# First stage of a two-layer decoder trunk: input, sixteen modulation rows and the first weights in one DRAM array

## The chip, the cores and the metric

The kernel runs on one core of a Trainium2 chip. The metric is the device time of one execution in microseconds (us). Five engines work side by side, each on its own queue: TensorE (PE in the profile, with its weight loads as PEld), VectorE (DVE), ScalarE (ACT), GpSimd (POOL) and SyncE (SP), which here issues nearly all DMAs. Engines wait for each other and for DMAs through semaphores.

## The reference

A trunk of two layers for one sequence of 256 tokens and model width 1024. Each layer is a half-step SwiGLU block, a token mixer (stick-breaking attention in layer 0, an RG-LRU recurrence in layer 1), and another half-step SwiGLU block; each of them starts from a normalised input that is scaled and shifted by a conditioning vector.

```python
mod = (c_act @ mod_w[layer] + mod_b[layer]).reshape(B, N_SUB, 3, D_MODEL)
shift, scale, gate = mod_j[:, 0], mod_j[:, 1], mod_j[:, 2]
h = rmsnorm(x, g) * (1 + scale[:, None, :]) + shift[:, None, :]
g, u = jnp.split(h @ w_gu, 2, axis=-1)
x = x + MACARON_W * (1 + gate) * ((jax.nn.silu(g) * u) @ w_down)
```

Only the very first block matters here: it needs the input `x` (1 MB), the conditioning vector `c`, the shift and scale of sub-layer 0 (two products of `c` with a 1024 x 1024 matrix of `mod_w`) and the weights `w_gu`.

## The kernel before, in words

The input is held transposed: 8 tiles `x[d]` of 128 rows of the model dimension by 256 tokens, in one buffer in on-chip memory (SBUF). Weights are float32. Each weight piece is loaded into `raw` (three buffers of 8 KB a partition), split by ACT into a rounded part `wh` (L555) and by DVE into the rest `wl` (L558), and multiplied in three passes by `Acc.group` (L584). The modulation is not computed by TensorE: each 128 x 1024 tile of the transposed `mod_w` is loaded, and one DVE instruction multiplies it by the activated vector and sums along the row (`mod_tile`, L616). One such tile gives one column, the 128 shifts or scales of one `x[d]`.

The order of work is not written by hand. The program lists its operations with costs and dependences; `Program.schedule` simulates the engines and sorts the operations by their simulated start. The costs of DMAs come from the size alone (`c_dma`), and the address is no part of it. A chain of `after` dependences (`chained`, and `last` in `early`) fixes the order of the first stage's DMAs on SP's queue. Every transfer is recorded by the helper `dma` and so has line L521.

The first stage reads, on SP's queue, in this order: the input in two halves (the second half carries 72 columns of parameters behind each row), the first scale tile (`w` = 1) and the first shift tile (`w` = 0), and then for each of the eight steps k of the model dimension the 128 x 2048 weights `gu0[k]`, in 512-column pieces for k = 0, 1, 3 and 7 and in 1024-column pieces for the others. Each half of a step's weights is followed by a modulation tile of the next step (for k up to 4), scale after the first half and shift after the second; for k of 5 and 6 both follow the first half. While this runs, ACT forms the two modulation columns `mf`, then the modulated input `hx` and `hpre` of step k (L528); DVE forms the rest of it (L907); TensorE multiplies it into eight banks, one for each of the first eight tiles of the hidden dimension. The first half of the weights of step 0 is multiplied unsplit (L883). Eight DMAs of SP can be on the way: a further one waits for the one issued eight before it.

Where these sources lie: `xT` is one array of 128 rows of 2120 columns, and each half is a column range of it. `modw` is an array of 2 x 72 tiles, each 128 x 1024 and contiguous; the 16 tiles of the first stage are two runs of 8. `gu0` holds for each k a contiguous 128 x 2048 block, and a piece is a column range of it: rows of 2 KB or 4 KB, 8 KB apart.

After the first stage the kernel streams the remaining weights in 1 MB loads and multiplies them; it takes some 95% of the time and isn't touched by the change.

Of the kernel before, what the change touches and what calls it, by code (L numbers as in the profile page):

```python
# [14 lines left out]
P = 128  # L15
T = 256
TX = T + 2
D = 1024
KD = D // P
# [10 lines left out]
CH = 2048  # L30
HALF = 1024
SQ = 8
NFIRST = 2
LAT0, RATE0, RATE = 1250.0, 390.0, 360.0
LAT1 = 2050.0
LASTY = 900.0
SMALL = (0,1,3,7)
# [15 lines left out]
NP0 = OFF_MB + 3 * KD  # L53
# [312 lines left out]
        return sorted(order, key=lambda o: o.start)  # L366


def c_act(n, psum=False, ptr=0):
    return (51.0 if psum else 93.0) + 0.8333 * n + 93.0 * ptr  # L370

# [11 lines left out]


@with_exitstack
def trunk(ctx, tc, xT, cb, par, modw, gu0, gu, wdn, qk, wv, wo, win, wri, wout, out):
    nc = tc.nc
    act, dve, pe, pool, sp = nc.scalar, nc.vector, nc.tensor, nc.gpsimd, nc.sync
    ctx.enter_context(tc.manual_schedule())
# [84 lines left out]
    xall = fixed("x", KD * T + NPAR)  # L474
    x = [Buf(ap=xall[:, d * T : (d + 1) * T]) for d in range(KD)]
    cact = Buf(ap=fixed("cact", D))
    pars = Buf(ap=xall[:, KD * T :])
# [42 lines left out]
    def dma(dst, src, n, w, after=(), lat=None, rate=RATE):  # L520
        return pr.op("DMA", c_dma(n, rate), lambda: sp.dma_start(dst(), src), w=w, after=after, lat=lat)  # L521
# [12 lines left out]
    def load(src, n, name, chain=None, size=HALF, plain=0, homes=(), behind=(), kind=Buf):  # L534


        homes = list(homes)
        raw = Buf(rawr, name=f"raw_{name}")
        part = None
        if chain is None:  # L540
            dma(lambda: raw()[:, :n], src, n, [raw])
        res = []
        for a in range(0, n, size):
            m = min(n - a, size)
            if chain is not None:
                part = a
                chain(lambda a=a, m=m: raw()[:, a : a + m], src[:, a : a + m], m, [(raw, a)])
            if len(res) < plain:
                res.append((raw, part))
                continue  # L550
            h, lo = (Set(homes.pop(0), 9) if homes else kind(ring_, name=f"{w}_{name}")
                     for ring_, w in ((whr, "wh"), (wlr, "wl")))

            def fh(h=h, a=a, m=m):
                act.activation(h()[:, :m], raw()[:, a : a + m], AF.Copy)  # L555

            def fl(h=h, lo=lo, a=a, m=m):
                dve.tensor_tensor(lo()[:, :m], raw()[:, a : a + m], f32(h()[:, :m]), ALU.subtract)  # L558

            pr.op("ACT", c_act(m), fh, [(raw, part)], [h], behind if res else ())  # L560
            V(fl, m, [(raw, part), h], [lo])
            res.append((h, lo))
        return res
# [45 lines left out]
    def mod_tile(l, s, w, t, after=(), lat=None, rate=RATE, home=None, behind=()):  # L609

        m = mraw[l, s, w]
        raw = home or Buf(modr)
        load_ = dma(raw, modw[l, (s * 3 + w) * KD + t], D, [raw], after, lat, rate)

        def fn():
            dve.scalar_tensor_tensor(raw(), raw(), 1.0, cact(), ALU.mult, ALU.mult, accum_out=m()[:, t : t + 1])  # L616
        V(fn, D, [raw, cact] + list(behind), [raw, (m, t)])
        return load_
# [226 lines left out]
    def ffn(l, s, nxt, hook):  # L845
# [12 lines left out]
        if j == 0:  # L858
# [3 lines left out]
            q = rstd((0, 0))  # L862
# [49 lines left out]
            for k in range(KD):  # L912
                if k == 0:
                    h0 = norm_chunk((0, 0), k, q, PLAIN > 0)
                    warm(LATE, [pr.last_pe])
                    for ks in xq_parts[:2]:
                        normed(ks)
                    copied = ()
                else:
                    copied = [first_chunk(k)]  # L920
                size = HALF // 2 if k in SMALL else HALF
                done = [0]

                def chain(dst, src, n, w):
                    chained(dst, src, n, w, RATE0, LAT0 if k < 3 else LAT1)
                    done[0] += n

                    if done[0] % HALF == 0:
                        for w in ((2 - done[0] // HALF,) if k < 5 else (1, 0) if done[0] == HALF else ()):
                            early(k + 1, w)  # L930

                plain = PLAIN if k == 0 else 0
                ws = load(gu0[k], CH, f"gu0_{k}", chain, size, plain, (), copied if k == 1 else ())
                if k == 1:
                    normed(xq_parts[2], [ws[0][1].hist[None][0]])
                other = copies(*hcur[0, 0][k]) if k in COPIED else None
                for f in range(SQ):
                    h = other if other and f == 2 else hcur[0, 0][k]
                    for g in range(2):
                        i, c0 = divmod((f * 2 + g) * P, size)  # L940
                        if i < plain:
                            plain_group(accs[f], g, *ws[i], (f * 2 + g) * P)
                            continue
                        group(accs[f], (g, 0), lambda b, g=g: b[:, g * T : (g + 1) * T], ws[i],
                              lambda u, c0=c0: u[:, c0 : c0 + P], h, lambda v: v[:, :T], T, k == KD - 1)
                        if k in KICK0 and f == g == 0:
                            kick_op(accs[f], 0, (0, 0))
# [439 lines left out]
    def chained(dst, src, n, w, rate=RATE, lat=LAT0):  # L1387
        last[:] = [dma(dst, src, n, w, last, lat, rate)]
# [10 lines left out]
    def first_loads(F):  # L1399
        c, b = Buf(modr), [Buf(banks), Buf(banks)]  # L1400
        act_dma(lambda: c()[:1, :], cb, [], [c], 300.0)

        def cond(h, after=()):
            cs = slice(h * 512, (h + 1) * 512)
            A(lambda: cact()[:, cs], b[h], AF.Silu, 512, [b[h]], [(cact, h)], table="silu", psum=True, after=after)

        warm(EARLY)
        for h in range(2):
            cs = slice(h * 512, (h + 1) * 512)
            pr.op("PE", 1870.0, lambda h=h, cs=cs: pe.matmul(b[h]()[:, :], ones[:1, :], c()[:1, cs], start=True, stop=True),  # L1410
                  [c], [b[h]])
        cond(0)
        warm(MID, [pr.last_pe])


        pairs = []
        for h, (scalar_, vector_, extra) in enumerate(((0, 2, 0), (2, 0, NP0))):
            d = 4 * h
            a0, n = d * T, 4 * T + extra
            chained(lambda a0=a0, n=n: xall[:, a0 : a0 + n], xT[:, a0 : a0 + n], n, x[d : d + 4] + [(pars, 0)] * h, RATE0)  # L1420
            sq = Buf(F, 8)
            v0 = vector_ * T
            V(lambda sq=sq, a0=a0, v0=v0: dve.tensor_tensor(
                sq()[:, v0 : v0 + 2 * T], xall[:, a0 + v0 : a0 + v0 + 2 * T], xall[:, a0 + v0 : a0 + v0 + 2 * T], ALU.mult),
              2 * T, x[d + vector_ : d + vector_ + 2], [(sq, "V")])
            for i in (scalar_, scalar_ + 1):
                o = A(lambda sq=sq, i=i: sq()[:, i * T : (i + 1) * T], x[d + i], AF.Square, T, [x[d + i]], [(sq, i)])
            if h == 1:
                cond(1, [o])
            p = Buf(F, 4)  # L1430
            V(lambda sq=sq, p=p: dve.tensor_tensor(p(), sq()[:, : 2 * T], sq()[:, 2 * T :], ALU.add), 2 * T,
              [(sq, "V"), (sq, scalar_), (sq, scalar_ + 1)], [p])
            if h == 0:
                pairs += [(p, slice(0, T)), (p, slice(T, 2 * T))]
            else:
                one = Buf(F, 2)
                fold = V(lambda p=p: dve.tensor_tensor(one(), p()[:, :T], p()[:, T:], ALU.add), T, [p], [one])
                pairs.append((one, slice(0, T)))
        ssq[0, 0] = tuple(pairs)
        pr.op("DVE", 80.0, lambda: dve.scalar_tensor_tensor(gbias(), col(OFF_MB + KD, KD), 1.0, col(OFF_NG, KD), ALU.add,  # L1440
                                                            ALU.mult), [(pars, 0)], [gbias], [fold])
# [4 lines left out]
    rate = {0: (1.4, SQ, 30), 1: (1.25, 0, 8), 2: (1.3, 0, 32), 3: (1.3, 0, 32)}  # L1446
# [38 lines left out]
def _layout(i):  # L1485
# [9 lines left out]
        [cols(i[n]) for n in ("norm_g", "mod_b", "final_norm_g", "lru_conv_w", "lru_conv_b", "lru_b_r", "lru_b_i",  # L1495
                              "lru_lambda")], axis=1)
    a["par"] = c(par[:, NP0:])
    a["xT"] = c(np.concatenate([i["x"].reshape(T, KD, P).transpose(2, 1, 0).reshape(P, KD * T), par[:, :NP0]], axis=1))
    a["modw"] = c(i["mod_w"].transpose(0, 2, 1)).reshape(2, 9 * KD, P, D)
    gu = i["ffn_w_gu"].reshape(4, KD, P, 2, NF, P)  # L1500
    a["gu0"] = c(gu[0, :, :, :, :SQ].transpose(0, 1, 3, 2, 4)).reshape(KD, P, SQ * 2 * P)
    a["gu"] = c(gu.transpose(0, 4, 2, 1, 3, 5)).reshape(4, NF, P, CH)
    a["wdn"] = c(i["ffn_w_down"].reshape(4, NF, P, D).transpose(0, 2, 1, 3))
    w = i["sb_w_qkv"].reshape(KD, P, 3, 8, P)
# [8 lines left out]
    return a  # L1513


_INS = ["xT", "cb", "par", "modw", "gu0", "gu", "wdn", "qk", "wv", "wo", "win", "wri", "wout"]


# [18 lines left out]
```

## Time and profile before

| | |
|---|---|
| time, median of 3 runs | 952.83 us (952.3 to 954.18) |
| profiled execution | 953.6 us |
| its span, first to last instruction | 951.9 us |
| TensorE busy | 940.5 us (99%) |
| DVE busy | 794.6 us (83%) |
| ACT busy | 571.0 us (60%) |
| DMA over the span | 251.25 MB, mean 264 GB/s |
| granted TensorE clock | 0.998 |

Times in the profile count from the first instruction. A row of a group or of the timeline gives line, engine, operation, output and inputs by their names in the program, and in brackets how long the engine stood idle before it and what ended that. In the list of waits a row gives who waited for whom, us in total, how many times, and the longest. The chain of waits follows back from the last instruction to whatever released it, step by step.

### The profile page before, as it was taken

What the parts mean: (1) busy time and instruction counts of PE and PEld (TensorE: products, weight loads), DVE (VectorE), ACT (ScalarE), POOL (GpSimd) and SP (SyncE); (2) the same over time, 40 slices, a digit from 0 to 9 for tenths busy, and PEclk for the clock granted to TensorE, in tenths of its full rate; (3) what the DMA queues carried; (4) which work ended last, traced back from release to release, by engine and by line L of the source; (5) the groups of instructions that cost most, each with busy time, mean ns of one, the idle gap of its engine ahead of it and who ended that gap; (6) DMA issues with size and microseconds to landing.
All of it is one profiled execution on the core that took longest, in us unless ns stands there. A gap on an engine that the chain in (4) does not pass through costs nothing.

```text
span 951.9 us, 19735 instructions
## 1 busy us (share of the span) xinstructions
PE 940.5 (99%) x8114; PEld 929.4 (98%) x8114; DVE 794.6 (83%) x1301; ACT 571.0 (60%) x936; POOL 2.4 (0%) x15
## 2 busy tenths in 40 slices
PE   8999999999999999999999999999999999999997
PEld 6999999999999999999999999999999999999996
DVE  7899988799989999888889989875998997555443
ACT  6685544478897855554467554535789676444333
POOL 1000000000000000000000000000000000000000
PEclk9999999999999999999999999999999999999999
DMA  9979999947745599989967998996243646545431
GB/s 343 403 288 362 366 348 349 362 177 278 279 146 179 193 340 352 348 307 349 367 231 288 346 335 335 331 350 252 90 166 145 222 166 245 209 178 201 170 118 45
DMA packets 48332, 251.25 MB, mean 264 GB/s; under 512 B 5361, under 2 KB 5745, under 8 KB 28530
## 3 DMA queue, kind: packets, MB, share of 16 engines
q1 hardware_dynamic: 47952, 249.59, 70.5%
q8 instruction: 63, 1.03, 0.4%
q10 hardware_dynamic: 290, 0.40, 0.1%
q14 instruction: 27, 0.22, 0.1%
HBM read 248.92 MB, written 1.05 MB: 263 GB/s over the span
## 4 chain that ended last, share of the span: by engine, by line
PE 93%; DMA 3%; DVE 2%; ACT 1%; issue 0%; SPq 0%; DVEq 0%
PE bank L584 87%; DMA raw<-in_gu 3%; PE bank L1004 2%; PE bank L1263 1%; PE bank L1152 1%; DVE wl L558 1%; DMA arenar<-in_modw 1%; PE bank L1092 1%; PE bank L1122 1%; DVE arenar L616 0%; ACT wh L555 0%; DVE x L1375 0%; PE bank L1125 0%; PE bank L1076 0%; DVE arenaf L1347 0%
## 5 line engine op out<-in xcount | busy, mean ns | idle before, releaser
L584 PE MATMUL bank<-hx,wh 128*128 128x256 f32 (+1 forms) x3280 | 564.1, 277 | 0.9 <-DVE hx L907 0.9
L555 ACT ACTIVATE wh<-raw 128x1024 fp32r<-128x1024 f32 (+1 forms) x330 | 336.4, 1040 | 286.8 <-PE bank L584 203.9
L584 PEld LDWEIGHTS bank<-hx,wh 128*128 128x128 f32 x3280 | 495.5, 188 | 1.5 <-DVE hx L907 1.5
L558 DVE TENSOR_TENSOR wl<-raw,wh 128x1024 fp32r<-128x1024 f32 (+1 forms) x330 | 388.1, 1197 | 108.2 <-ACT wh L555 105.5
L584 PE MATMUL bank<-hx,wl 128*128 128x256 f32 (+1 forms) x1648 | 456.4, 277 | 0.5 <-DVE wl L558 0.5
L584 PEld LDWEIGHTS bank<-hx,wl 128*128 128x128 f32 x1648 | 309.8, 188 | 0.8 <-DVE wl L558 0.7
L584 PE MATMUL bank<-arenar,wh 128*128 128x256 f32 x1696 | 289.4, 276 | 0.0
L584 PEld LDWEIGHTS bank<-arenar,wh 128*128 128x128 f32 x1696 | 255.3, 188 | 0.0
L584 PE MATMUL bank<-arenar,wl 128*128 128x256 f32 x848 | 234.3, 276 | 0.1
L616 DVE SCALAR_TENSOR_TENSOR rawm<-rawm,cact 128x1024 f32<-128x1024 f32 x128 | 155.1, 1219 | 15.3 <-DMA rawm<-in_modw 15.1
L584 PEld LDWEIGHTS bank<-arenar,wl 128*128 128x128 f32 x848 | 159.3, 188 | 0.3 <-DVE wl L558 0.3
L528 ACT ACTIVATE arenar<-a 128x256 fp32r<-128x256 f32 x88 | 35.2, 405 | 9.2 <-DVE a L838 7.5
L843 DVE TENSOR_TENSOR arenar<-a,arenar 128x256 fp32r<-128x256 f32 x88 | 36.2, 417 | 0.5 <-ACT arenar L528 0.5
L528 ACT ACTIVATE sg<-bank 128x256 f32<-128x256 f32 x82 | 29.9, 369 | 6.8 <-PE bank L584 6.7
L838 DVE TENSOR_TENSOR a<-bank,sg 128x256 f32<-128x256 f32 x82 | 33.8, 416 | 0.1
L753 DVE SCALAR_TENSOR_TENSOR x<-bank,mf,x 128x256 f32<-128x256 f32 (+1 forms) x49 | 21.7, 472 | 9.2 <-PE bank L584 9.1
L528 ACT ACTIVATE hx<-x,mf 128x256 fp32r<-128x256 f32 x40 | 19.3, 500 | 14.6 <-DVE x L753 14.6
L528 ACT ACTIVATE hx<-hpre,mf 128x256 fp32r<-128x256 f32 x41 | 20.0, 503 | 10.2 <-DVE hpre L700 9.8
L1004 PE MATMUL bank<-wh,hx 128*128 128x256 f32 x128 | 23.4, 281 | 0.0
L528 ACT ACTIVATE arenaf<-bank 128x512 f32<-128x512 f32 (+1 forms) x37 | 17.1, 508 | 5.9 <-PE bank L1125 2.0
L1480 ACT ACT_TABLE_LOAD x15 | 19.2, 1283 | 1.6 <-PEq L1525 1.3
L1004 PEld LDWEIGHTS bank<-wh,hx 128*128 128x128 f32 x128 | 20.0, 188 | 0.1
(128 smaller groups left out, 542.7 us busy)
## 6 DMA issues: line engine op xcount, KB each, us to landing
raw<-in_gu SPq DMA_DIRECT2D x79, 1024.0 KB, 5.9
rawm<-in_modw SPq DMA_DIRECT2D x128, 512.0 KB, 7.3
raw<-in_wdn SPq DMA_DIRECT2D x44, 1024.0 KB, 5.3
raw<-in_win SPq DMA_DIRECT2D x10, 1024.0 KB, 5.0
arenar<-in_modw SPq DMA_DIRECT2D x16, 512.0 KB, 9.2
raw<-in_qk SPq DMA_DIRECT2D x8, 1024.0 KB, 4.9
raw<-in_gu SPq DMA_DIRECT2D x10, 512.0 KB, 8.6
raw<-in_wout SPq DMA_DIRECT2D x5, 1024.0 KB, 5.0
```

What stands on the lines that cost most here:

```text
L528: act.activation(o(), i(), f, **{k: (v() if callable(v) else v) for k, v in kw.items()})
L555: act.activation(h()[:, :m], raw()[:, a : a + m], AF.Copy)
L558: dve.tensor_tensor(lo()[:, :m], raw()[:, a : a + m], f32(h()[:, :m]), ALU.subtract)
L584: pe.matmul(o(b()), wc(u()), xc(v()), start=start and n == 0, stop=stop and n == len(passes) - 1, skip_group_check=True)
L616: dve.scalar_tensor_tensor(raw(), raw(), 1.0, cact(), ALU.mult, ALU.mult, accum_out=m()[:, t : t + 1])
L753: dve.scalar_tensor_tensor(x[d]()[:, w], acc.b()[:, j * T + w.start : j * T + w.stop], gate()[:, d : d + 1], x[d]()[:, w], ALU.mult, ALU.add)
L838: V(lambda: dve.tensor_tensor(a(), b()[:, T:], sg(), ALU.mult), T, [(b, (1, 0)), sg], [a])
L843: V(lambda: dve.tensor_tensor(y[1](), a(), f32(y[0]()), ALU.subtract), n, [a, y[0]], [y[1]])
L1004: pe.matmul(o, u()[:, tb * P : (tb + 1) * P], v()[:, c0 : c0 + 256], start=start and n == 0, stop=k == KD - 1 and n == 2, skip_group_check ...
L1092: pe.matmul(zb[e][i]()[:, j * m : (j + 1) * m], v()[rows, kc], w()[rows, qc], start=False, stop=j == 1 and n == 2, skip_group_check=True)
L1122: pe.matmul(b()[:, : NC[i]], ntri, blk(q(), i), start=False, stop=i == j == 1, skip_group_check=True)
L1480: act.preload_act_table_set(TABLES[t])
```

## The change

Input, the sixteen modulation tiles of the first stage and all pieces of `gu0` are packed into one flat DRAM array `first_in`, 17.9 MB, by the host before the launch. `first_order` lists the pieces: the two halves of the input, then for each k the scale tile, the shift tile and the weight pieces of that step. Each piece is contiguous there, row behind row. The kernel walks the same list to find each piece's offset (`at_`), and the DMAs take their source from it. The arrays `xT` and `gu0` are gone; `modw` stays whole, and its first 16 tiles of shift and scale are now read from the copy. Destinations, sizes and the order of the DMAs are as before. The order in the array and the order on the queue differ a little: on the queue the modulation tiles of step k lie among the pieces of step k − 1.

```diff
+def piece(k):
+    return HALF // 2 if k in SMALL else HALF
+
+
+def first_order():
+
+    yield "x", 0, 0, 4 * T
+    yield "x", 4, 0, 4 * T + NP0
+    for k in range(KD):
+        yield "m1", k, 0, D
+        yield "m0", k, 0, D
+        for a in range(0, CH, piece(k)):
+            yield "gu", k, a, piece(k)
...
+    at_ = {}
+    for *key, n in first_order():
+        o = sum(P * q.shape[1] for q in at_.values())
+        at_[tuple(key)] = first_in[o : o + P * n].rearrange("(p n) -> p n", n=n)
...
-                chain(lambda a=a, m=m: raw()[:, a : a + m], src[:, a : a + m], m, [(raw, a)])
+                chain(lambda a=a, m=m: raw()[:, a : a + m], src[a // size] if isinstance(src, list) else src[:, a : a + m], m, [(raw, a)])
...
-        load_ = dma(raw, modw[l, (s * 3 + w) * KD + t], D, [raw], after, lat, rate)
+        src = at_[f"m{w}", t, 0] if (l, s) == (0, 0) and w < 2 else modw[l, (s * 3 + w) * KD + t]
+        load_ = dma(raw, src, D, [raw], after, lat, rate)
...
-                ws = load(gu0[k], CH, f"gu0_{k}", chain, size, plain, (), copied if k == 1 else ())
+                ws = load([at_["gu", k, a] for a in range(0, CH, size)], CH, f"gu0_{k}", chain, size, plain, (), copied if k == 1 else ())
...
-            chained(lambda a0=a0, n=n: xall[:, a0 : a0 + n], xT[:, a0 : a0 + n], n, x[d : d + 4] + [(pars, 0)] * h, RATE0)
+            chained(lambda a0=a0, n=n: xall[:, a0 : a0 + n], at_["x", d, 0], n, x[d : d + 4] + [(pars, 0)] * h, RATE0)
...
+    src = {"x": lambda k: xT[:, k * T :], "gu": lambda k: g0[k], "m0": lambda k: a["modw"][0, k],
+           "m1": lambda k: a["modw"][0, KD + k]}
+    a["first_in"] = np.concatenate([src[what](k)[:, o : o + n].reshape(-1) for what, k, o, n in first_order()])
```

More of the change, by code (lines that the diff above doesn't have):

```diff
@@ L385, in trunk @@
 @with_exitstack
-def trunk(ctx, tc, xT, cb, par, modw, gu0, gu, wdn, qk, wv, wo, win, wri, wout, out):
+def trunk(ctx, tc, first_in, cb, par, modw, gu, wdn, qk, wv, wo, win, wri, wout, out):
+    at_ = {}
+    for *key, n in first_order():
+        o = sum(P * q.shape[1] for q in at_.values())
+        at_[tuple(key)] = first_in[o : o + P * n].rearrange("(p n) -> p n", n=n)
     nc = tc.nc
@@ L920, in ffn @@
                     copied = [first_chunk(k)]
-                size = HALF // 2 if k in SMALL else HALF
+                size = piece(k)
                 done = [0]
@@ L1497, in _layout @@
     a["par"] = c(par[:, NP0:])
-    a["xT"] = c(np.concatenate([i["x"].reshape(T, KD, P).transpose(2, 1, 0).reshape(P, KD * T), par[:, :NP0]], axis=1))
+    xT = np.concatenate([i["x"].reshape(T, KD, P).transpose(2, 1, 0).reshape(P, KD * T), par[:, :NP0]], axis=1)
     a["modw"] = c(i["mod_w"].transpose(0, 2, 1)).reshape(2, 9 * KD, P, D)
     gu = i["ffn_w_gu"].reshape(4, KD, P, 2, NF, P)
-    a["gu0"] = c(gu[0, :, :, :, :SQ].transpose(0, 1, 3, 2, 4)).reshape(KD, P, SQ * 2 * P)
+    g0 = gu[0, :, :, :, :SQ].transpose(0, 1, 3, 2, 4).reshape(KD, P, CH)
+    src = {"x": lambda k: xT[:, k * T :], "gu": lambda k: g0[k], "m0": lambda k: a["modw"][0, k],
+           "m1": lambda k: a["modw"][0, KD + k]}
+    a["first_in"] = np.concatenate([src[what](k)[:, o : o + n].reshape(-1) for what, k, o, n in first_order()])
     a["gu"] = c(gu.transpose(0, 4, 2, 1, 3, 5)).reshape(4, NF, P, CH)
@@ L1513, in _layout @@
     return a
-_INS = ["xT", "cb", "par", "modw", "gu0", "gu", "wdn", "qk", "wv", "wo", "win", "wri", "wout"]
+_INS = ["first_in", "cb", "par", "modw", "gu", "wdn", "qk", "wv", "wo", "win", "wri", "wout"]
 def kernel(**inputs):
```

## The prediction

> **What bounds the kernel now.** I read the page first, then the list of who waited for whom on PE over the whole run, then the chain of waits of the first 70 us, then a table of short stretches of the first stage.
>
> ```profile
> span 951.9 us, 19735 instructions
> ...
> PE 93%; DMA 3%; DVE 2%; ACT 1%; issue 0%; SPq 0%; DVEq 0%
> ```
>
> The chain that ends last is 93% TensorE; 3% of 951.9 us, some 29 us, hangs on DMA. The next view says where TensorE ever stood still for another engine:
>
> ```profile
> PE bank L883 <- ACT hpre L528: 1.4, 1, 1.4
> PE bank L1396 <- POOL eps L481: 1.2, 1, 1.2
> PE bank L584 <- DVE hx L907: 0.9, 3, 0.4
> PE bank L584 <- DVE wl L558: 0.5, 1, 0.5
> PE bank L1410 <- DMA rawm<-in_cb: 0.4, 1, 0.4
> ```
>
> That is the whole list. The 1.2 and 0.4 lie in the first microseconds, the 1.4 right before the first real product (L883); of the two L584 rows all four waits lie in the first stage. So there are two things to win: an earlier first product, and 0.9 + 0.5 = 1.4 us of waits behind it. Nothing else in the run waits for a load in such a way that TensorE stops.
>
> The chain of waits of the first stage shows that those waits come from DMA:
>
> ```profile
> 7.90 8.20 DMA raw<-in_gu
> ...
> 16.11 9.95 DMA raw<-in_gu
> ...
> 26.13 7.77 DMA raw<-in_gu
> ```
>
> From 7.90 to 33.90 us the chain is three transfers, one behind the other. The table of stretches (columns: stretch and length, busy time of PE, PEld, DVE, ACT, POOL with counts, granted clock, DMA share, GB/s) shows the queue full and at what rate it runs:
>
> ```profile
> 2.00:5.00 3.00, 2.64 (x4) 1.16 (x4) 1.56 (x5) 1.00 (x2) 1.08 (x6) 1.00 0.87 335
> 5.00:6.00 1.00, 1.00 (x2) 0.00 (x0) 0.22 (x2) 1.00 (x4) 0.00 (x0) 1.00 1.03 355
> 6.00:7.50 1.50, 1.50 (x6) 1.05 (x6) 1.40 (x3) 1.48 (x4) 0.00 (x0) 1.00 1.00 401
> 7.50:11.50 4.00, 3.24 (x14) 1.95 (x13) 3.71 (x9) 2.11 (x5) 0.00 (x0) 1.00 0.94 290
> 11.50:15.50 4.00, 3.32 (x15) 2.96 (x16) 3.34 (x8) 2.45 (x5) 0.00 (x0) 1.00 1.05 411
> 15.50:23.00 7.50, 7.50 (x65) 7.41 (x64) 7.00 (x12) 5.17 (x10) 0.00 (x0) 1.00 1.03 405
> 23.00:31.00 8.00, 7.08 (x60) 6.69 (x59) 6.54 (x9) 5.25 (x12) 0.00 (x0) 1.00 1.03 399
> 31.00:36.60 5.60, 5.27 (x46) 5.08 (x45) 5.60 (x10) 3.60 (x8) 0.00 (x0) 1.00 1.03 410
> 36.60:39.10 2.50, 2.50 (x23) 2.41 (x22) 2.50 (x5) 1.49 (x4) 0.00 (x0) 1.00 1.03 411
> 39.10:41.70 2.60, 2.60 (x25) 2.60 (x25) 2.60 (x4) 1.99 (x4) 0.00 (x0) 1.00 1.02 405
> 41.70:44.30 2.60, 2.60 (x25) 2.60 (x25) 1.69 (x4) 2.57 (x3) 0.00 (x0) 1.00 1.04 411
> 45.00:47.00 2.00, 2.00 (x19) 1.98 (x19) 2.00 (x4) 0.79 (x2) 0.00 (x0) 1.00 1.04 392
> ```
>
> The DMA engines are busy all the time and move about 400 GB/s, with one hole: 290 GB/s from 7.5 to 11.5 us. What moves then follows from counting bytes in the order of issue: 2 to 7.5 us moved 1.00 + 0.36 + 0.60 = 1.96 MB; the input is 1.09 MB and the first two modulation rows 1.05 MB. So the hole begins about where the first rows of `gu0` are read, in pieces of 2 KB a partition out of rows of 8 KB. The other half of the same 1 MB, with the same pitch and the same pieces, falls into 11.5 to 15.5 us and runs at 411. The pitch alone is therefore not the reason; a first read of that array could be. A smaller dip (355) stands where the first modulation row, the first read of `modw`, begins.
>
> **The change part by part.** No engine's instructions are added, removed or moved: each of the five queues has the same operations with the same shapes in the same order (the written order comes from a planner whose costs know sizes and not addresses), and SP issues the same DMAs with the same waits. Nothing is queued behind a new wait. The packing is done on the host before the launch and costs no device time. What is left is 42 source addresses on SP's queue: two DMAs of input, 16 modulation rows and 24 pieces of `gu0`, 17.9 MB in all (1.09 + 8.39 + 8.39). I count three effects.
>
> (a) The hole. 4.00 us at 290 GB/s are 1.16 MB, which at the 411 of the next stretch take 2.82 us: 1.18 us. The dip at 5 to 6 us is worth 1.00 − 0.355/0.411 = 0.14 us. If they come from the first read of another array, one array takes them away; if they come from the moment, or from first reading any new memory, nothing goes. Bounds 0 and 1.32 us.
>
> (b) The pitch. By the same count of bytes 36.6 to 39.1 and 41.7 to 44.3 carry modulation rows, which lie contiguous already (411 and 411), 39.1 to 41.7 carries 4 KB pieces out of 8 KB rows (405), 45 to 47 carries 2 KB pieces out of 8 KB rows (392). Four of the eight steps have 4 KB pieces: 4.19 MB, 10.35 us at 405 and 10.20 at 411, so 0.15 us. Contiguous 2 KB pieces are in no row of this trace; the nearest is the 4 KB pair, the same 1.5% and another 0.16 us. Bounds 0 and 0.3; a loss is the second rival.
>
> The Trainium skill ("DMA: Bandwidth & Descriptors", section on latency and other measured facts) advises padding the row pitch or laying tiles out contiguously, for pitches from 512 KiB (207 GB/s) to 4 MiB (103); for the 8 KB here the trace shows only the 405 against 411.
>
> (c) The number and size of packets. It stays, for SBUF still takes one row a partition; the row for 36.6 to 39.1 us, contiguous modulation rows, shows it:
>
> ```profile
> DMA packets 283, 1.03 MB, mean 411 GB/s; under 512 B 32, under 2 KB 32, under 8 KB 283
> ```
>
> 1.03 MB over the 251 packets of 512 B and more is 4.1 KB, one partition's row. So contiguity gains nothing here: 0.
>
> What of a lead of the transfers reaches the end? TensorE's waits show the way:
>
> ```profile
> 21.99 1.06 ACT L555 ACTIVATE wh<-raw 128x1024 fp32r<-128x1024 f32 x1 [1.05 <-DMA raw<-in_gu]
> ...
> 24.88 0.38 PE L584 MATMUL bank<-hx,wh 128*128 128x256 f32 x1 [0.38 <-DVE hx L907]
> ...
> 26.15 1.06 ACT L555 ACTIVATE wh<-raw 128x1024 fp32r<-128x1024 f32 x1 [1.78 <-DMA raw<-in_gu]
> ...
> 28.53 0.39 PE L584 MATMUL bank<-hx,wl 128*128 128x256 f32 x1 [0.54 <-DVE wl L558]
> ```
>
> ACT works in order; while it waits for raw at 21.99 the scaling column and hx of the next step stand behind it, which costs TensorE 0.38 at 24.88. The landing at 26.1 costs it 0.54 at 28.53 by way of wh and wl; the other two waits for hx make 0.9 − 0.38 = 0.5. TensorE has no slack before them, so a lead of the transfers is won one for one until 1.4 us are used up; beyond that DVE, busy 5.60 of 5.60 us in 31 to 36.6, is late next. After the stage TensorE waits for nothing, so the gain goes to the end whole.
>
> The first product is not moved by it:
>
> ```profile
> 8.34 1.22 DVE L616 SCALAR_TENSOR_TENSOR arenar<-arenar,cact 128x1024 f32<-128x1024 f32 x1
> ...
> 9.57 1.22 DVE L616 SCALAR_TENSOR_TENSOR arenar<-arenar,cact 128x1024 f32<-128x1024 f32 x1
> ...
> 12.18 0.48 PE L883 MATMUL bank<-hpre,raw 128*128 128x256 f32 x1 [1.44 <-ACT hpre L528]
> ```
>
> DVE reduces the first two modulation rows back to back (neither row shows a wait for the DMA), so their landing earlier moves nothing; the weights of that product are covered by this chain. Bounds 0 and 0.3 us; I take 0.
>
> Sum: of (a) I take 0.9, three quarters of the upper bound without the small dip, because the half of the same block that follows shows the full rate and the hole sits at the change of array; of (b) 0.1. A lead of 1.0 us, under 1.4, so 1.0 off the profiled execution: 953.6 − 1.0 = 952.6. That execution lies 0.8 above the median of 952.83, and the lowest run (952.3) lies 1.3 below it, about as much as all four waits; an ordinary run probably waits less. Off the median I take 0.8: 952.0 us. Own range of this case 951.3 to 952.6.
>
> **The rivals.**
>
> *Nothing.* The hole stays, because it belongs to the moment or to memory that is read for the first time in whatever array; the stage is at its ceiling of about 411 in every other stretch. For it: in steady alternation of the two arrays (15.5 to 23 us, 405) changing array costs nothing that shows. Also the new array is not quite in the order of reading: a step's modulation rows lie in front of its pieces but are read between those of the step before. Time 952.8, within 0.3 either way. The Trainium skill ("DMA: Bandwidth & Descriptors", section on why a DMA increments its semaphore by 16) says that one descriptor moves one contiguous run of the last dimension, by which longer contiguous memory changes nothing; the packet row agrees.
>
> *Slower.* Pieces that lie densely are read more slowly: the rows of a 2 KB piece then stand 2 KB apart instead of 8. The place is the full queue from 11.5 to 46 us, 34.5 us in which each lost per cent of rate is 0.35 us on the path, without a cover. It decides from 0.2% of the time, 1.9 us, that is 5.5%: 405 down to 383 GB/s. For it: the 2 KB pieces are the slowest stretch (392), and contiguous ones are not shown. Against it: the contiguous 4 KB rows are the fastest (411). At 5.5 to 9% 954.7 to 955.9.
>
> *Clearly faster.* All four waits go (1.4) and the first product comes 0.5 earlier, more than the bound above allows: 950.9 or less. Against it stands the unbroken DVE chain from 8.34 us.
>
> **How the numbers follow.** Forecast 0.50, nothing 0.20, slower 0.17, clearly faster 0.13. 0.2% (1.9 us) is about what a measurement of this kernel can tell from no change. The first two cases lie within it: 0.70; faster 0.13, slower 0.17. The range 950.8 to 955.0 takes in the first two, the upper end of the gain and the nearer half of the slower case, and leaves out about 0.2.
>
> **What would show it.** In the changed kernel the stretch 7.5 to 11.5 us should move 380 GB/s or more, and the waits of L584 for hx and wl sum to 0.6 or less. The nothing case shows 290 again in that stretch and 1.4 of waits; the slower one rates under 390 between 11.5 and 46 us and longer waits of ACT for raw. The forecast fails if the hole moves with the first rows of the weights, if a wait on DVE takes the place of each that goes, or if the first product starts at another time than 12.2.

## The result and the profile after

The changed kernel takes 951.62 us in the median of 17 runs (950.83 to 952.40); the kernel before, run beside it, 952.69 us (17 runs, 952.08 to 954.18). The ratio is 0.9986, with a 95% interval from 0.998 to 0.9993: faster by 0.14%, about 1.1 us, and inside the 0.2% that the prediction counts as "the same". The profiled execution took 951.2 us with a span of 949.5 us.

The table of stretches of the changed kernel, cut as in the prediction:

```profile
2.00:5.00 3.00, 2.82 (x4) 1.16 (x4) 1.65 (x5) 1.17 (x3) 1.07 (x6) 1.00 1.00 370
5.00:6.00 1.00, 1.00 (x2) 0.00 (x0) 0.31 (x1) 1.00 (x5) 0.00 (x0) 1.00 1.02 410
6.00:7.50 1.50, 1.50 (x6) 1.17 (x6) 1.40 (x3) 1.48 (x3) 0.00 (x0) 1.00 0.99 403
7.50:11.50 4.00, 3.80 (x14) 2.19 (x12) 3.72 (x9) 2.01 (x6) 0.00 (x0) 1.00 1.05 408
11.50:15.50 4.00, 3.52 (x17) 3.13 (x17) 4.00 (x9) 2.89 (x6) 0.00 (x0) 1.00 1.03 399
15.50:23.00 7.50, 7.50 (x67) 7.44 (x67) 7.12 (x14) 6.19 (x12) 0.00 (x0) 1.00 1.03 406
23.00:31.00 8.00, 8.00 (x73) 8.00 (x72) 7.94 (x12) 4.84 (x9) 0.00 (x0) 1.00 1.03 402
31.00:36.60 5.60, 5.60 (x52) 5.56 (x51) 5.57 (x10) 4.18 (x7) 0.00 (x0) 1.00 1.03 408
```

The hole is gone: 408 GB/s (last column) where 290 stood. In 23 to 31 us PE (second figure) is busy for all 8.00 us, before 7.08. Behind 11.5 us the rates are those of before. The list of who waited for whom on PE, the whole run of the changed kernel:

```profile
PE bank L1416 <- POOL eps L500: 1.2, 1, 1.2
PE bank L903 <- ACT hpre L547: 0.7, 1, 0.7
PE bank L1430 <- DMA rawm<-in_cb: 0.2, 1, 0.2
PE bank L603 <- DVE hx L927: 0.2, 1, 0.2
```

Three of the four waits behind the first product (L903 here, L883 before) are gone: 1.4 us became 0.2. But the span fell by 2.4 us, from 951.9. The list for the weight loads shows more of it. Of the kernel before:

```profile
PEld bank L883 <- ACT hpre L528: 1.7, 1, 1.7
PEld bank L584 <- DVE hx L907: 1.5, 3, 0.6
...
PEld bank L584 <- DVE wl L558: 1.0, 2, 0.7
```

and of the changed kernel:

```profile
PEld bank L903 <- ACT hpre L547: 1.0, 1, 1.0
...
PEld bank L603 <- DVE hx L927: 0.4, 1, 0.4
...
PEld bank L603 <- DVE wl L577: 0.3, 1, 0.3
```

The waits behind the first product (`hx` and `wl`) went from 2.5 us to 0.7, so 1.8 us of them went; the 0.3 us left for `wl` lies behind the first stage in both kernels. The PE rows show less, because a matmul beside such a wait is shown as longer: the two behind waits in the prediction's lines have 0.38 and 0.39 us, where the mean is 0.28. The wait for `hpre`, 1.7 and 1.0 us, is no measure of a gain: the first product starts only 0.2 us earlier (12.18 and 11.98), and the matmuls on zeros that fill the time ahead of it end at 10.7 before and 11.3 after. The start times of the same matmul, counted through the run, say where the time was won (us from the start of the span, the first matmul at 1.16 in all three; "again" is the second profile of the unchanged kernel, below):

```
matmul no.    before     again     after
   40          15.31     15.10     15.11
  120          25.44     25.32     24.42
  160          30.80     29.86     28.96
  200          35.94     34.47     33.49
  320          50.26     48.79     47.56
 last         944.66    943.19    942.30
```

All of it is won ahead of matmul 320: 2.7 us against the first profile, 1.2 against the second. Behind it nothing is won, and 0.3 us is lost again in both comparisons, far from the change (between matmuls 6400 and 6600, some 760 us into the run); no wait shows why. Of the 2.7 us the rows of waits account for 2.0 (1.8 and 0.2). The second column also shows that the first profile of the kernel before was one of its slower executions.

### The profile page after: what moved, and what is told of

Same layout as the page of the kernel before. It is cut to its first block, busy times and chain, and to the rows that moved or that the text cites. A ratio compares the mean times of both kernels' runs of the same rounds, so it can differ in the third digit from the quotient of the medians.

```text
span 949.5 us, 19735 instructions
## 1 busy us (share of the span) xinstructions
PE 940.3 (99%) x8114; PEld 929.6 (98%) x8114; DVE 793.9 (84%) x1301; ACT 571.1 (60%) x936; POOL 2.4 (0%) x15
## 2 busy tenths in 40 slices
DMA packets 48332, 251.25 MB, mean 265 GB/s; under 512 B 5361, under 2 KB 5745, under 8 KB 28530
## 4 chain that ended last, share of the span: by engine, by line
PE 93%; DMA 3%; DVE 2%; ACT 1%; issue 0%; SPq 0%; DVEq 0%
PE bank L603 87%; DMA raw<-in_first_in 3%; PE bank L1024 2%; PE bank L1283 1%; PE bank L1172 1%; DMA arenar<-in_first_in 1%; DVE wl L577 1%; PE bank L1112 1%; PE bank L1142 1%; DVE arenar L636 0%; ACT wh L574 0%; DVE x L1395 0%; PE bank L1145 0%; PE bank L1096 0%; DVE arenaf L1367 0%
```

## The experiments

Where an experiment is judged by one execution's rate in 7.5 to 11.5 us, the row of the table of stretches is shown. Beside them I use the trace's records of single packets, put to their DMAs by size and order: the mean duration of the 128 packets of a DMA. For the 2 KB pieces 84 ns is the undisturbed value. The ratios are against the kernel before, run beside each group of experiments; its medians there were 952.97 us (e0 to e3), 952.99 (e4 to e7) and 952.82 (e8 to e11).

```
mean ns of a packet          step 0,  step 0,  step 1,
                             piece 1  piece 2  piece 1
before / again               159/130  111/108    84/84
after                             84       84       85
e1_dense                          84       84       86
e2_onearray                      190       94       84
e3_gap                            84       84       86
e4_step0                          87       84      137
e5_rest                          154      121       84
e6_rowpad, 9 KB                   84       84       86
e7_xdense                        104      104       84
e8_pad256, 8448 bytes             84       84       86
e9_pitch16k                      136      121       84
e10_disturb                      107       89       85
e11_reversed                      84       84       86
```

The same records give the cost of the hole as a time. From the first packet of step 0 to the first of step 1 there pass 5.20 to 5.22 us in the changed kernel, e1, e3, e6, e8 and e11, 6.2 in both profiles of the kernel before, e2 and e5, and 6.0 in e9: the hole holds the queue up by 0.8 to 1.0 us. In e7 and e10 it is 5.5.

**The kernel before once more (e0).** No edit.

> The kernel before, unchanged, profiled a second time. If the hole belongs to where the data lies, 7.5 to 11.5 us moves about 290 GB/s again (under 330) and 5 to 6 us about 355. If it was an accident of one execution, 7.5 to 11.5 us moves 380 or more. Time 952.1 to 954.2 us either way.

```profile
5.00:6.00 1.00, 1.00 (x2) 0.00 (x0) 0.51 (x2) 0.81 (x4) 0.00 (x0) 1.00 0.98 384
...
7.50:11.50 4.00, 3.92 (x14) 2.16 (x12) 3.72 (x9) 2.28 (x6) 0.00 (x0) 1.00 0.87 289
```

The hole belongs to the kernel: 289 GB/s again. The small dip at 5 to 6 us does not: 384 here, 355 in the first profile. Time 952.61 us, ratio 0.9996 (0.9986 to 1.0006). This execution, with the same hole, waited less behind it: its span is 950.4 us.

**Contiguous pieces in three arrays (e1).**

```diff
-                ws = load(gu0[k], CH, f"gu0_{k}", chain,
+                w0 = gu0[k].rearrange("p n -> (p n)")
+                ws = load([w0[P * a_ : P * (a_ + size)].rearrange("(p n) -> p n", n=size) for a_ in range(0, CH, size)], CH, f"gu0_{k}", chain,
```

> Three arrays as before, but every piece of gu0 contiguous in its own array. Theory 'array' (the first read of a further DRAM array is slow): the hole stays, 7.5 to 11.5 us under 330 GB/s, 5 to 6 us about 355, time 952.7 us. Rival 'pitch' (pieces out of 8 KB rows are slow when first read): 7.5 to 11.5 us at 390 or more, and most of the gain, 951.8 us; 5 to 6 us stays at 355 under both.

```profile
7.50:11.50 4.00, 3.81 (x14) 2.20 (x13) 3.72 (x9) 2.13 (x5) 0.00 (x0) 1.00 1.04 401
```

**One array, rows as long as before (e2).**

```diff
+    for key, n in [("x", KD * T + NP0)] + [(q, n) for k in range(KD) for q, n in ((("m", 1, k), D), (("m", 0, k), D), (("gu", k), CH))]:
+        at_[key] = first_in[o_ : o_ + P * n].rearrange("(p n) -> p n", n=n)
+        o_ += P * n
...
-                ws = load(gu0[k], CH, f"gu0_{k}", chain,
+                ws = load(at_["gu", k], CH, f"gu0_{k}", chain,
```

> One array in the order of reading, but the input and the gu0 blocks keep their rows (8480 bytes and 8 KB), so every piece is a column range as before. Theory 'array': no hole, 7.5 to 11.5 us at 390 GB/s or more, 951.7 us. Rival 'pitch': hole as before, under 330, 952.7 us. The input's start (2 to 5 us: 335 before, 370 after) tells whether its 8480-byte pitch mattered: 335 if yes, 370 if no.

```profile
7.50:11.50 4.00, 3.47 (x12) 1.98 (x11) 3.70 (x8) 3.14 (x7) 0.00 (x0) 1.00 0.96 284
```

These two decide the main question. Contiguous pieces without the common array give 951.37 us, ratio 0.9986 (0.9977 to 0.9994), the whole gain; the common array without contiguous pieces gives 952.88 us, ratio 1.0004 (0.9993 to 1.0016), and the hole. My theory, the first read of a further array, has fallen, and the pitch carries the change. Two things came out otherwise than expected. In e1 the stretch 5 to 6 us moved 408 GB/s, where both theories had 355. In e2 the stretch 2 to 5 us moved 326, which fits the case that the input's 8480-byte rows matter; e7 below tests that. And the time of e2 is a weaker witness than its rate: in its profiled execution the second half of the input came late (`arenaf`, a wait of 0.5 us) and the matmuls of the first product started 0.43 us apart at first instead of 0.22, so that TensorE stood 2.5 us later at matmul 40 than in the kernel before. e1, and the longer rows below, carry the point on time.

**A gap inside the array (e3).**

```diff
         o = sum(P * q.shape[1] for q in at_.values())
+        o += GAP * (len(at_) >= 4)
```

> The changed kernel with 64 MB of unread memory in the same array between the first shift tile and the first weights. Theory 'array': a gap inside one array changes nothing, 7.5 to 11.5 us at 390 GB/s or more, 951.6 us. Rival 'distance' (the first read of memory far from what was read so far is slow, whatever array): the hole is back, under 340, and 952.4 us or more.

```profile
7.50:11.50 4.00, 3.04 (x14) 1.81 (x12) 3.72 (x9) 1.99 (x6) 0.00 (x0) 1.00 1.05 404
```

951.29 us, ratio 0.9988 (0.998 to 0.9996). 64 MB of distance cost nothing that shows.

That leaves the question why the same 8 KB rows are read at full rate from the third piece on.

**Only step 0 contiguous (e4), and all but step 0 (e5).** One edit with two lists of steps (`DENSE` is `(0,)` and then 1 to 7):

```diff
+                w0, src = gu0[k].rearrange("p n -> (p n)"), gu0[k]
+                if k in DENSE:
+                    src = [w0[P * a_ : P * (a_ + size)].rearrange("(p n) -> p n", n=size) for a_ in range(0, CH, size)]
+                ws = load(src, CH, f"gu0_{k}", chain,
```

> Three arrays; only the four pieces of step 0 are contiguous, steps 1 to 7 stay column ranges out of 8 KB rows. Theory 'first block' (only the first weights suffer from the pitch): no hole anywhere, 7.5 to 11.5 and 11.5 to 15.5 us both at 390 GB/s or more, time as with all pieces contiguous, 951.4 us. Rival 'in step' (engines that have run in step so far collide on the first pitched piece that comes, and once they are out of step no more): the hole moves to step 1, 7.5 to 11.5 us over 380 but 11.5 to 15.5 us under 360, time about 952.5 us.

Two stretches with only step 0 contiguous:

```profile
7.50:11.50 4.00, 4.00 (x17) 2.71 (x15) 3.86 (x8) 2.38 (x5) 0.00 (x0) 1.00 1.03 405
11.50:15.50 4.00, 2.75 (x14) 2.28 (x13) 3.75 (x10) 2.89 (x7) 0.00 (x0) 1.00 1.04 367
```

> The reverse: step 0 out of 8 KB rows, steps 1 to 7 contiguous. Both theories: the hole as before, 7.5 to 11.5 us under 330 GB/s, 952.7 us. Were the gain of 0.14% spread over the steady stretch (contiguous pieces 1.5% faster, as the prediction had it with 0.1 to 0.3 us), 952.4 us and 15.5 to 45 us some GB/s above before.

With all but step 0:

```profile
7.50:11.50 4.00, 4.00 (x15) 2.41 (x13) 3.72 (x8) 2.20 (x5) 0.00 (x0) 1.00 0.95 291
```

The hole moved to the first pitched piece that is left: 137 ns a packet in step 1, 84 in the kernel before, and 367 GB/s in its stretch (under 360 was expected). It is shallower than in step 0. So it isn't the first block's data that is slow, but the first pieces with 8 KB rows, in both places tried. Times: 952.28 us, ratio 0.9991 (0.9982 to 0.9999), and 952.89 us, ratio 0.9991 (0.9978 to 1.0004); intervals too wide to tell these two apart. The profiled execution of e4 also began late, with a wait of 1.1 us for the conditioning vector (`in_cb`) and the first product at 12.93 us, so its time is not the price of the moved hole alone.

**Rows of 9 KB (e6), of 8448 bytes (e8) and of 16 KB (e9)** instead of 8 KB (`ROWPAD` 256, 64 and 2048 columns, never read):

```diff
+    a["gu0"] = c(np.concatenate([g0, np.zeros((KD, P, ROWPAD), np.float32)], axis=2))
```

> The kernel before with gu0's rows 1 KB longer (unread), so that pieces are read out of 9 KB rows. If the hole needs a pitch that is a power of two: 7.5 to 11.5 us at 390 GB/s or more, 951.5 us. If any pitch larger than the piece does it: under 330 and 952.7 us.

> The kernel before with gu0's rows 256 bytes longer (pitch 8448 bytes). If the hole needs rows that fall on the same place of a power of two: either it goes as with 1 KB (7.5 to 11.5 us at 390 GB/s or more, 951.7 us), so that one step of 256 bytes is enough, or, if neighbouring rows must be further apart, it stays partly (300 to 370, 952.3 us).

> The kernel before with gu0's rows twice as long (pitch 16 KB, half unread). Power-of-two theory: the hole stays, 7.5 to 11.5 us at 290 GB/s or less, and may be longer; 952.8 us or more. If something else about 8 KB rows did it, 390 or more and 951.7 us.

With 9 KB:

```profile
7.50:11.50 4.00, 3.56 (x14) 2.09 (x12) 3.72 (x9) 2.23 (x6) 0.00 (x0) 1.00 1.04 401
```

With 8448 bytes:

```profile
7.50:11.50 4.00, 3.40 (x14) 2.00 (x13) 3.72 (x9) 2.25 (x5) 0.00 (x0) 1.00 1.04 401
```

With 16 KB:

```profile
7.50:11.50 4.00, 3.59 (x14) 2.12 (x13) 3.72 (x9) 2.12 (x5) 0.00 (x0) 1.00 0.95 301
```

951.84 us, ratio 0.9987 (0.9978 to 0.9996); 951.47 us, 0.9985 (0.9976 to 0.9995); and 953.11 us, 1.0004 (0.9995 to 1.0013). The pieces need not be contiguous: 256 unread bytes behind each row bring the whole gain, and double rows none. (301 GB/s with 16 KB lies a little above the 290 or less that was expected.) Of the four row lengths tried only the two powers of two show the hole. A power of two is not enough by itself: contiguous 2 KB pieces have rows 2 KB apart and show none (84 ns). What sets 8 and 16 KB apart from 2 KB no run shows. The Trainium skill ("DMA: Bandwidth & Descriptors", section on latency and other measured facts) lists a loss of this kind for pitches from 512 KiB on and infers streams in lock step that meet on the same memory channel. The runs agree in kind, at 8 and 16 KB; they do not show the channels.

**The input contiguous, nothing else (e7).**

```diff
-            chained(lambda a0=a0, n=n: xall[:, a0 : a0 + n], xT[:, a0 : a0 + n], n, x[d : d + 4] + [(pars, 0)] * h, RATE0)
+            chained(lambda a0=a0, n=n: xall[:, a0 : a0 + n], xT[a0 * P : (a0 + n) * P].rearrange("(p n) -> p n", n=n), n, x[d : d + 4] + [(pars, 0)] * h, RATE0)
```

> The kernel before with the two halves of the input each contiguous, nothing else changed. If the input's 8480-byte rows cost its start: 2 to 5 us at 360 GB/s or more (before 335 and 339), hole unchanged (under 330), 952.4 us. If not: 2 to 5 us at 335 to 345 and 952.7 us.

```profile
5.00:6.00 1.00, 1.00 (x2) 0.00 (x0) 0.06 (x1) 0.91 (x3) 0.00 (x0) 1.00 0.72 136
...
7.50:11.50 4.00, 3.39 (x15) 2.06 (x13) 3.72 (x8) 2.71 (x6) 0.00 (x0) 1.00 1.00 363
```

Both expectations missed the hole, which is shallower here (363). This execution had a deep dip (136 GB/s) just before it, which no other profile shows as deep; so the engines may have come to the weights out of step. A dip alone is no proof of that: e5 moved 326 in the same microsecond and kept its whole hole. The stretch 2 to 5 us moved 353, between the two expectations; over all profiles a contiguous input gave 331 to 370 there and a pitched one 326 to 346. Time 952.48 us, ratio 0.9996 (0.9987 to 1.0005); the input's layout shows no gain.

**Some DMA engines put behind (e10).** The test of that idea, three small reads ahead:

```diff
+        for i in range(3):
+            d = Buf(modr)
+            act_dma(lambda d=d: d()[:8, :], modw[1, 8 + i][:8, :], [], [d], 300.0)
```

> The kernel before with three small extra reads on ACT's queue at the start (8 rows of 4 KB each, unused), which should put some of the DMA engines about 0.5 us behind the others before the first weights; 8 KB rows unchanged. Theory 'in step': the hole is shallower, 7.5 to 11.5 us over 330 GB/s although more bytes are to be moved. If being in step has nothing to do with it: 290 as before. Time is no test of either: the engines that are put behind land later, 952.5 to 953.5 us.

```profile
6.00:7.50 1.50, 1.50 (x6) 1.04 (x6) 0.58 (x1) 0.00 (x0) 0.00 (x0) 1.00 0.96 306
7.50:11.50 4.00, 3.23 (x10) 1.80 (x10) 3.82 (x7) 3.09 (x6) 0.00 (x0) 1.00 1.01 375
```

375 GB/s with 8 KB rows unchanged, and 107 and 89 ns a packet instead of 130 to 159 and 108 to 111. That speaks for engines in step; part of the loss has moved ahead, to 306 in 6 to 7.5 us, so it is support and no proof. The edit also changed more than it was to: SP issued the third and fourth piece of step 0 at 7.54 and 7.91 us (4.24 and 4.74 before), and no view shows which DMA engine moved which packet, so that some engines were put behind is not shown. 953.2 us, ratio 1.0003 (0.9993 to 1.0012).

**The array in the reverse order of reading (e11).**

```diff
-    for *key, n in first_order():
+    for *key, n in reversed(list(first_order())):
```

> The changed kernel with the pieces in the array in the reverse order of reading, each still contiguous. If the order of reading in the array matters: slower than the changed kernel, 952.3 us or more. If only the pitch counts: the same, 7.5 to 11.5 us at 390 GB/s or more, 951.6 us.

```profile
7.50:11.50 4.00, 4.00 (x14) 2.71 (x13) 3.86 (x7) 2.39 (x5) 0.00 (x0) 1.00 1.04 403
```

No hole. The median, 952.27 us, ratio 1.0002 (0.9989 to 1.0015), is where "order matters" had put it; the interval takes in no gain at all and just leaves out the full one (0.9986). The profiled execution, 958.14 us, lost some 6 us between 450 and 730 us, where both kernels read the same sources and TensorE was busy throughout, so not by waiting for a load. It also began late, with a wait of 1.2 us for `in_cb` (0.2 in the changed kernel) and the first product at 13.00 us; `in_cb` is no part of the array. Whether the order costs something besides stays open.

## Why the prediction was right or wrong

The time (952.0 forecast, 951.62 measured), the direction and the size (0.8 off the median forecast, 1.1 measured) were right. That they came out in spite of a wrong cause is luck: the change put everything into one array and, beside that, made every piece contiguous, and only the second did the work. Term by term:

- *(a) the hole.* That it goes, and that most of its 1.18 us are won: right (290 to 408 GB/s; 0.9 taken, 1.0 by the packets from step 0 to step 1). The reason was wrong. The step that failed is "the pitch alone is therefore not the reason", drawn from the second half of the block, which ran at 411 with the same pitch. The runs show that the pitch is the reason: pieces out of 8 or 16 KB rows are slow, but only the first of them that are read, so the full rate of the second half proved nothing. The array, which I put in its place, does nothing that shows (e1, e2, e3). The 0.14 us for the dip at 5 to 6 us was a swing between executions: 355 and 384 in the two profiles of the kernel before.
- *(b) the pitch in the steady stretch.* 0.1 us taken, bounds 0 to 0.3: no sign of it. The comparison of 405 with 411 GB/s was within the variation: the changed kernel, contiguous throughout, has 399 to 408 in the rows shown behind 11.5 us. Nor do the 2 KB pieces of the last step, in the slowest stretch before (392 in 45 to 47 us), run faster when contiguous: 86 to 88 ns a packet before, 86 to 89 after. In e5, contiguous from step 1 on, 15.5 to 36.6 us has 405, 403 and 407, against 405, 399 and 410 before.
- *(c) packets.* Right: 48332 on both pages.
- *TensorE's waits.* "One for one until 1.4 us are used up" failed by its cap: in the weight loads' rows the waits of the first stage behind the first product are 2.2 us, not 1.4, and 1.8 of them went. It also failed as "one for one" in the profile it was read from: the first packet of step 1 came 1.3 us later there than in the changed kernel (13.84 and 12.52), and TensorE lost 2.5 us behind the first product. In the second profile of the kernel before it holds: 1.1 us (13.64) and 1.2. The forecast did not suffer, since the prediction reckoned that another execution has less to win and took 0.8 off the median.
- *The first product.* 12.18 us before, 11.98 after: 0.2, inside the bounds of 0 to 0.3. The second profile of the kernel before has 11.97, so 0, as taken, fits as well.
- *The rivals.* Nothing: excluded by the interval. Slower: contiguous 2 KB rows are not slower (84 ns a packet, 408 GB/s). Clearly faster: did not come, as the chain from 8.34 us hardly moved.

What stays open is the mechanism below the pitch. That engines in step meet in memory fits e4, e7 and e10 and the three longer rows, but it is argued, not shown: no row names the engines or the place where they meet.

## What to carry to other kernels

When a DMA queue that is on the path reads column ranges out of rows whose length is a power of two (8 and 16 KB here), look at the rate of its first microseconds, and try 256 unread bytes behind each row before rebuilding the layout. A layout change does several things at once: undo them one by one, since here the visible one (one array in reading order) did nothing and a side effect (other row lengths) did all. Look for TensorE's waits at its weight loads too, and let the start times of the same matmul in both profiles decide.

## What the runs showed that was not expected

- Rows of 8 KB and 16 KB, read in 2 KB pieces, ran at 284 to 301 GB/s for 4 us at the start of the stream and at 409 to 415 in the next 4; rows of 8448 bytes or 9 KB ran at 401 from the start. In two runs with something else ahead of the weights the 8 KB rows had 363 and 375.
- A gap of 64 MB, or another array, costs nothing that shows at its first read (404 and 401 GB/s).
- Two profiled executions of the same kernel with the same hole differ by 1.5 us in span (951.9 and 950.4), all of it in the first stage, between the first product and matmul 320 but for 0.2 ahead of it.
